# A seventh product in place of eight for SwiGLU's first pair, and a bank seeded by ScalarE

## The chip, the cores and the metric

The kernel runs on one core of one Trainium2 chip. The metric is the device time of one execution in microseconds (us), the median of several; one execution is profiled on its own. TensorE is called PE (PEld is its weight load), VectorE DVE, ScalarE ACT, GpSimd POOL, SyncE SP.

## What is computed

One layer of an encoder block on x of 512 tokens by 1024 features, all float32:

```python
h = rmsnorm(x, g_mix); proj = h @ w_in                       # 1024 -> 11264 columns
y_a = (gb * dwconv3(gc * xc)) @ w_a_out                      # gated short convolution
y_r = (groupnorm(retention(q, k, v)) * g_ret * silu(g_sw)) @ w_r_out
x = x + (sigmoid(gate_a) * y_a + sigmoid(gate_r) * y_r) @ w_o
h2 = rmsnorm(x, g_ffn)
x = x + (silu(h2 @ w_ff_gate) * (h2 @ w_ff_up)) @ w_ff_down  # 1024 -> 2816 -> 1024
return rmsnorm(x, g_final)
```

The stretch that matters here is the last matmul of the mixer (w_o) and the SwiGLU that follows it.

## The kernel before

Every float32 operand is held as two parts, hi and lo; a product of tiles is three matmuls (hi by hi, hi by lo, lo by hi). `split` makes the parts: ACT copies hi, then DVE subtracts it from the source to get lo (L171, L172).

Most matrix products go by a scheme of seven products in place of eight: a quad is a two by two arrangement of blocks of the weights (b11, b12, b21, b22) and of the activations. The seven weight units, in `FORMS`, are b11, t1, t2, b21, t3, t4, b22; t1 to t4 are sums of two blocks, and each of them costs one more DVE add (L244) ahead of its split. On the side of the activations four sums s1 to s4 are formed (`sums`, L602), four adds and four splits. `fm_quad` (the convolution's columns), `strassen` (the other projections and the down projection) and `pair` (SwiGLU's gate and up columns) each run the seven products into three banks of PSUM, called a, d and b: b11 into a, which ACT copies out as p1; t1 into d; t2 on top of a, copied out as u2; b21 into b, and DVE then adds p1 to it; t3 on top of a, copied out as u3; t4 on top of a; b22 on top of d. A product that adds to bank a can't start before the copy of a has read it.

SwiGLU has eleven such quads q = 0 to 10 of 256 gate and 256 up columns, and three parts of the down projection, after q = 2, 6 and 10 (`FF_PARTS`). One product of a SwiGLU quad is one call of `prod`: 24 matmuls of 128 x 256. The first quad is different: `first_pair` (L983) computes its eight products plainly from the four blocks, since the products for the first 256 tokens can start before the last quarter of the tokens has been turned (`tr_o`) and the sums s1 to s4 exist. For q = 1 `begin` and `second` (the products of b11 and b21) stand ahead of `pair`; for later quads `second(q)` stands between the products of t2 and t3, and `begin(q + 1)` between those of t3 and t4.

The weights come in the order of `PLAN`. `load_raws` issues the DMAs on SP's queue, `LEAD` = 4 units ahead, into ten raw buffers; `prefetch_form` makes the sum, if there is one, in place in its raw buffer, and splits it into one of five pairs of buffers (`wpool`); `take` hands the next unit out and keeps two more on the way (`AHEAD`).

The order in which each engine gets its instructions is not the text's: a planner sorts them ahead of time, by the order of the text, by what is ready by its own clock and by which buffers are free. So an add or a split for a later quad can stand ahead of work that the text puts first, and matmuls of one product between those of another.

Of the kernel before, what the change touches and what calls it, by code (L numbers as in the profile page):

```python
# [21 lines left out]
NB = S // P  # L22
# [33 lines left out]
def plan():  # L56
# [47 lines left out]

    f(0, "b11", "b21", "b12", "b22")
    f(1, "b11", "b21")
    for q0, n in FF_PARTS:
        for q in range(max(q0, 1), q0 + n):
            f(q, *(x for x in FORMS[1:5] if q > 1 or x != "b21"))
            if q + 1 < NQ:  # L110
                f(q + 1, "b11")
            f(q, "t4", "b22")
        units = [(name, u) for name in FORMS for u in range(0, n, 2)]
        if q0 + n == NQ:

            i = units.index(("b21", 2))
            units[i:i + 3] = units[i + 1:i + 3] + units[i:i + 1]
        for name, u in units:
            out.append(("q", ("d", q0), name, u, min(2, n - u)))
# [7 lines left out]
def loads():  # L127

    out = []
    for i, x in enumerate(PLAN):  # L130
        if x[0] == "q":
            _, quad, name, u, nk = x
            need = name if quad == ("f", 0) else NEEDS.get(name)
            if need:
                out.append((i, quad, need, u, nk * WIDTH[quad[0]]))
# [7 lines left out]
def block_kernel(ctx: ExitStack, tc: tile.TileContext, xT, xtok, wpack, wquad, cols, decs, rot, g_ffn, g_final, out):  # L143
# [173 lines left out]
    def prod(w, x, ps, start, stop=True):  # L317

        (wh, wl), (xh, xl) = w, x
        for s in range(2):  # L320
            o = ps[:, s * 256:(s + 1) * 256]
            for k in range(4):
                c = slice(k * 256 + s * P, k * 256 + (s + 1) * P)
                for i, (l, r) in enumerate(((wh, xh), (wh, xl), (wl, xh))):
                    nc.tensor.matmul(o, l[:, c], r[:, k], start=start and s == 0 and k == 0 and i == 0,  # L325
                                     stop=stop and k == 3 and i == 2, skip_group_check=True)

    def fm_quad(forms, ev11, ev21, ev22, ev12):

        def w():  # L330
            return take()[1][0]
        a, d, b = bank(), bank(), bank()
        prod(w(), forms["a11"], a, True)
        p1 = snap(a)
        prod(w(), forms["s1"], d, True)
        prod(w(), forms["s2"], a, False)
        u2 = snap(a)
        prod(w(), forms["a12"], b, True)
        nc.vector.tensor_tensor(out=p1, in0=b, in1=p1, op=ALU.add)
        ev11(p1)  # L340
        prod(w(), forms["s3"], a, False)
# [37 lines left out]
    def strassen(n, forms, ev11, ev21, ev22, ev12):  # L379


        a, d, b = ([bank(), bank()] for _ in range(3))
        prod_tm(n, forms["a11"], a, True)
        p1 = [snap(x) for x in a]
        prod_tm(n, forms["s1"], d, True)
        prod_tm(n, forms["s2"], a, False)
        u2 = [snap(x) for x in a]
        prod_tm(n, forms["a12"], b, True, True)
        for tt in range(2):
            nc.vector.tensor_tensor(out=p1[tt], in0=b[tt], in1=p1[tt], op=ALU.add)  # L390
            ev11(tt, p1[tt])
        prod_tm(n, forms["s3"], a, False)
# [58 lines left out]
    class SumSq:  # L451
# [18 lines left out]
        def rstd_tokens(self):  # L470
# [13 lines left out]
            for nb in range(NB):  # L484
                nc.vector.tensor_scalar_mul(diag[:, nb * P:(nb + 1) * P], ident, r[:, nb:nb + 1])
            self.diag = (t512(F32R), t512(F32R))
            split(diag, *self.diag)
            return r

        def rstd_row(self):  # L490

            ps = bank()
            nc.tensor.matmul(ps, ones_r, self.diag[0], start=True, stop=False)
# [131 lines left out]
    def do_quad(left, right, func, func_left=None):  # L625
# [6 lines left out]

        def ev21(tt, ps):
            t = t512()
            nc.scalar.activation(t, ps, func_left or AF.Copy)
            store(left[:, 2 + tt, :], t)
        strassen(4, xforms, ev_sum(left, 0, func_left), ev21, ev_sum(right, 2, func), ev_sum(right, 0, func))

# [289 lines left out]
    for nb in range(NB):  # L928
# [4 lines left out]
        if nb:  # L933
            tr_o(nb - 1, hs[nb - 1])
        hs[nb] = ev_o(nb, [po[half][nb] for half in range(2)])


# [44 lines left out]

    def first_pair():  # L983
        w = {}
        g0, u0, g1, u1 = bank(), bank(), bank(), bank()
        _, (w["b11"],) = take()
        prod(w["b11"], XF[0, 0], g0, True, False)
        _, (w["b21"],) = take()
        prod(w["b21"], XF[1, 0], g0, False)
        tr_o(NB - 1, hs[NB - 1])  # L990
        _, (w["b12"],) = take()
        prod(w["b12"], XF[0, 0], u0, True, False)
        _, (w["b22"],) = take()
        prod(w["b22"], XF[1, 0], u0, False)
        gated(0, 0, g0, u0)
        prod(w["b11"], XF[0, 1], g1, True, False)
        prod(w["b21"], XF[1, 1], g1, False)
        XF.update(sums(xf32[0, 0], xf32[1, 0], xf32[0, 1], xf32[1, 1]))
        prod(w["b12"], XF[0, 1], u1, True, False)
        prod(w["b22"], XF[1, 1], u1, False)  # L1000
        gated(0, 1, g1, u1)

    heads_of = {}

    def begin(q):
# [4 lines left out]
        prod(w, XF[0, 0], st["a"], True)  # L1010
        st["p1"] = snap(st["a"])

    def second(q):
        b = bank()
        _, (w,) = take()
        prod(w, XF[1, 0], b, True)
        g = heads_of[q]["p1"]
        nc.vector.tensor_tensor(out=g, in0=b, in1=g, op=ALU.add)

    def pair(q):  # L1020
# [12 lines left out]
        nc.vector.tensor_tensor(out=u3, in0=d, in1=u3, op=ALU.subtract)  # L1033
        if q + 1 < NQ:
            begin(q + 1)
# [16 lines left out]
    def down(n):  # L1052
        strassen(n, act_forms(), lambda tt, t: add_y(t, tt, 0), lambda tt, ps: add_y(snap(ps), 2 + tt, 0),
                 lambda tt, t: add_y(t, 2 + tt, 1), lambda tt, t: add_y(t, tt, 1))

    first_pair()
    begin(1)
    second(1)
    for q0, n in FF_PARTS:
        for q in range(max(q0, 1), q0 + n):  # L1060
            pair(q)
# [155 lines left out]
```

## Time and profile before

| | us |
|---|---|
| time, median of 3 runs | 1044.6 (1043.32 to 1044.88) |
| the profiled execution | 1043.97 |
| its span in the trace | 1042.2 |
| PE busy | 1028.3 (99%) |
| PEld busy | 897.0 (86%) |
| DVE busy | 875.5 (84%) |
| ACT busy | 523.4 (50%) |
| POOL busy | 107.7 (10%) |

The span is the trace's; the time of the execution has 1.8 us around it. The granted clock of PE is at its full share through the span but for the tail. SwiGLU's products begin at 702.06 us of the span; the eight of the first quad, with a turn of 1.00 us among them, end at about 726; the first part of the down projection begins at 769.53.

### The profile page before, as it was taken

The page shows a single profiled execution, that of the slowest core. Times are in us where ns is not written, and L with a number is a line of the kernel's source. Part 1 is how long each engine was busy: PE and PEld are TensorE (multiplying, and loading weights), DVE is VectorE, ACT ScalarE, POOL GpSimd, SP SyncE. Part 2 cuts the span into 40 slices and gives each one's busy share as a digit, 9 for nine tenths or more (in the row PEclk, how much of TensorE's full clock was granted, in tenths as well). Part 3 has the DMA queues.
Part 4 walks back from the last instruction along what each step waited for, and adds up shares of the span by engine and source line. Part 5 has one row for each costly group of instructions (what it writes and reads, how often), then busy time and mean ns, then how long its engine had stood idle before and what let it go on. Part 6 is the DMA issues. An engine that isn't in the chain of part 4 may idle for free.

```text
span 1042.2 us, 14832 instructions
## 1 busy us (share of the span) xinstructions
PE 1028.3 (99%) x5664; PEld 897.0 (86%) x5664; DVE 875.5 (84%) x1127; ACT 523.4 (50%) x698; POOL 107.7 (10%) x180
## 2 busy tenths in 40 slices
PE   8999999999999999999999999999999999999996
PEld 7788888888888998888888888889998999899985
DVE  6999786858787888697989998669998899889995
ACT  6546745452656545243443234355555565556553
POOL 0121111111111004202011000000002000110011
PEclk9999999999999999999999999999999999999999
DMA  9635638173645576919176535630319322663322
GB/s 325 223 117 201 236 123 281 71 254 119 199 141 182 169 284 233 341 42 358 42 283 247 205 111 173 236 113 28 92 45 275 117 85 78 193 152 102 122 35 87
DMA packets 49688, 175.07 MB, mean 168 GB/s; under 512 B 6480, under 2 KB 6480, under 8 KB 46288
## 3 DMA queue, kind: packets, MB, share of 16 engines
q1 hardware_dynamic: 36592, 131.12, 36.9%
q0 software_dynamic: 13024, 43.00, 12.9%
q8 instruction: 44, 0.72, 0.3%
q14 instruction: 28, 0.23, 0.1%
HBM read 135.56 MB, written 38.54 MB: 167 GB/s over the span
## 4 chain that ended last, share of the span: by engine, by line
PE 77%; issue 9%; DVE 7%; DMA 3%; POOL 2%; ACT 1%; SPq 0%; POOLq 0%; DVEq 0%; ACTq 0%
PE bank L369 29%; PE bank L325 27%; PE bank L285 7%; PE bank L284 7%; PE bank L286 7%; DVE wlo L172 1%; POOL z L566 1%; DVE big L185 1%; DMA big<-ql 1%; DMA big<-xT 1%; DMA z<-t 1%; DMA tab<-tab 0%; DVE big L172 0%; DVE t L464 0%; DVE big L175 0%
## 5 line engine op out<-in xcount | busy, mean ns | idle before, releaser
L171 ACT CAST whi<-raw 128x1024 fp32r<-128x1024 f32 (+1 forms) x281 | 288.6, 1032 | 302.7 <-PE bank L369 66.4
L172 DVE TENSOR_TENSOR wlo<-raw,whi 128x1024 fp32r<-128x1024 f32 (+1 forms) x281 | 335.8, 1202 | 108.8 <-ACT whi L171 107.8
L325 PE MATMUL bank<-xform,whi 128*128 128x256 f32 x1440 | 260.3, 283 | 0.0
L325 PEld LDWEIGHTS bank<-xform,whi 128*128 128x128 f32 x1440 | 224.8, 192 | 0.7 <-ACT t L376 0.6
L325 PE MATMUL bank<-xform,wlo 128*128 128x256 f32 x720 | 203.7, 283 | 0.0
L369 PE MATMUL bank<-whi,big 128*128 128x512 f32 x548 | 172.4, 390 | 0.0
L244 DVE TENSOR_TENSOR raw<-raw 128x1024 f32<-128x1024 f32 (+1 forms) x124 | 148.5, 1205 | 1.8 <-DMA raw<-wquad 0.4
L325 PEld LDWEIGHTS bank<-xform,wlo 128*128 128x128 f32 x720 | 138.2, 192 | 0.0
L369 PEld LDWEIGHTS bank<-whi,big 128*128 128x128 f32 x548 | 102.7, 188 | 22.4 <-DVE big L172 0.6
L369 PE MATMUL bank<-wlo,big 128*128 128x512 f32 x274 | 106.7, 389 | 0.0
L369 PE MATMUL bank<-whi,xform 128*128 128x512 f32 x320 | 101.2, 389 | 0.3 <-ACT t L376 0.3
L284 PE MATMUL bank<-whi,big 128*128 128x512 f32 x240 | 94.3, 395 | 1.8 <-ACT big L174 1.8
L285 PE MATMUL bank<-wlo,big 128*128 128x512 f32 x240 | 94.3, 393 | 0.0
L286 PE MATMUL bank<-whi,big 128*128 128x512 f32 x240 | 93.4, 392 | 0.0
L284 PE MATMUL bank<-big,whi 128*128 128x512 f32 x224 | 87.1, 389 | 0.0
L285 PE MATMUL bank<-big,whi 128*128 128x512 f32 x224 | 87.1, 389 | 0.0
L286 PE MATMUL bank<-big,wlo 128*128 128x512 f32 x224 | 87.1, 389 | 0.0
L376 ACT COPY t<-bank 128x512 f32<-128x512 f32 x96 | 55.5, 585 | 35.8 <-PE bank L369 17.2
L369 PEld LDWEIGHTS bank<-whi,xform 128*128 128x128 f32 x320 | 60.1, 188 | 13.1 <-ACT t L376 0.7
L369 PE MATMUL bank<-wlo,xform 128*128 128x512 f32 x160 | 62.2, 389 | 0.0
L369 PEld LDWEIGHTS bank<-wlo,big 128*128 128x128 f32 x274 | 51.4, 188 | 10.5
L284 PEld LDWEIGHTS bank<-whi,big 128*128 128x128 f32 x240 | 45.5, 190 | 12.5 <-ACT big L174 2.1
(173 smaller groups left out, 1398.6 us busy)
## 6 DMA issues: line engine op xcount, KB each, us to landing
raw<-wquad SPq DMA_DIRECT2D x124, 512.0 KB, 4.4
raw<-wpack SPq DMA_DIRECT2D x58, 512.0 KB, 4.9
z<-t POOLq DMA_DIRECT2D x24, 256.0 KB, 4.9
zform<-z POOLq DMA_DIRECT2D x6, 1024.0 KB, 6.2
v<-t POOLq DMA_DIRECT2D x16, 256.0 KB, 5.0
sg<-t POOLq DMA_DIRECT2D x16, 256.0 KB, 3.3
qh<-t POOLq DMA_DIRECT2D x16, 256.0 KB, 2.6
ql<-t POOLq DMA_DIRECT2D x16, 256.0 KB, 2.7
```

The costliest lines, as they stand in the source:

```text
L171: nc.scalar.copy(hi, src)
L172: nc.vector.tensor_tensor(out=lo, in0=src, in1=hi.bitcast(F32), op=ALU.subtract)
L185: nc.vector.transpose(o[:, :, :, b, :], i[:, :, :, q, :])
L244: nc.vector.tensor_tensor(out=t, in0=t, in1=raws[quad, more, u][:, 0:n], op=ALU.add)
L284: nc.tensor.matmul(ps, lh, rh, start=first, stop=False)
L285: nc.tensor.matmul(ps, lh, rl, start=False, stop=False)
L286: nc.tensor.matmul(ps, ll, rh, start=False, stop=last)
L325: nc.tensor.matmul(o, l[:, c], r[:, k], start=start and s == 0 and k == 0 and i == 0, stop=stop and k == 3 and i == 2, skip_group_check=True)
L369: nc.tensor.matmul(pss[tt], l, r[:, c], start=start and k == 0 and i == 0, stop=stop and k == n - 1 and i == 2, skip_group_check=True)
L376: nc.scalar.copy(t, ps)
L566: nc.gpsimd.dma_start(dst, t)
```

## The change

SwiGLU's quad 0 runs by seven products like the others. Ahead of it stand five products: b11 and b21 of quad 0, then (behind the last turn and the sums) b11 and b21 of quad 1, and b11 of quad 2; then `pair(0)` and `pair(1)`, each of five products with none of another quad in between in the text, then `pair(2)` with its seven as before. In every quad of the kernel (but the last part of the down projection, whose code stands apart) the product of b11 is now copied by ACT into the PSUM bank b (`seed`), and the product of b21 adds to that bank; DVE's add falls away, and what it fed reads the bank. For quads 0 to 2 of SwiGLU that bank is one that the w_o stage leaves. In the w_o stage two more units are fetched, after its second and its fourth block of tokens. The row of reciprocal norms at the start is made in the bank that its column was made in.

```diff
-    f(0, "b11", "b21", "b12", "b22")
+    f(0, "b11", "b21")
     f(1, "b11", "b21")
+    f(2, "b11")
     for q0, n in FF_PARTS:
-        for q in range(max(q0, 1), q0 + n):
+        for q in range(q0, q0 + n):
             f(q, *(x for x in FORMS[1:5] if q > 1 or x != "b21"))
-            if q + 1 < NQ:
+            if 1 < q < NQ - 1:
                 f(q + 1, "b11")
             f(q, "t4", "b22")
...
+    def seed(ps, t=None):
+        t = t or bank()
+        nc.scalar.copy(t, ps)
+        return t
...
-        a, d, b = bank(), bank(), bank()
+        a, d = bank(), bank()
         prod(w(), forms["a11"], a, True)
-        p1 = snap(a)
+        b = seed(a)
...
-        prod(w(), forms["a12"], b, True)
-        nc.vector.tensor_tensor(out=p1, in0=b, in1=p1, op=ALU.add)
-        ev11(p1)
+        prod(w(), forms["a12"], b, False)
+        ev11(b)
...
         def rstd_row(self):
-            ps = bank()
+            ps = self.ps
...
         hs[nb] = ev_o(nb, [po[half][nb] for half in range(2)])
+        if nb in (1, 3):
+            prefetch()
...
     def begin(q):
...
         prod(w, XF[0, 0], st["a"], True)
-        st["p1"] = snap(st["a"])
+        st["p1"] = seed(st["a"], (po[0][1], po[0][2], po[1][2])[q] if q < 3 else None)
     def second(q):
-        b = bank()
         _, (w,) = take()
-        prod(w, XF[1, 0], b, True)
-        g = heads_of[q]["p1"]
-        nc.vector.tensor_tensor(out=g, in0=b, in1=g, op=ALU.add)
+        prod(w, XF[1, 0], heads_of[q]["p1"], False)
     def pair(q):
...
-        if q + 1 < NQ:
+        if 1 < q < NQ - 1:
             begin(q + 1)
...
-    first_pair()
+    begin(0)
+    second(0)
+    tr_o(NB - 1, hs[NB - 1])
+    XF.update(sums(xf32[0, 0], xf32[1, 0], xf32[0, 1], xf32[1, 1]))
     begin(1)
     second(1)
+    begin(2)
     for q0, n in FF_PARTS:
-        for q in range(max(q0, 1), q0 + n):
+        for q in range(q0, q0 + n):
             pair(q)
```

`strassen` gets the same two edits as `fm_quad`, for both of its token tiles; `do_quad` and `down` evict the first result from PSUM by an ACT activation or copy, where they took it from SBUF.

## Rows read from the trace of the kernel before

**Rows 1.** The page's first part: engine, busy us, share, instructions.

```profile
PE 1028.3 (99%) x5664; PEld 897.0 (86%) x5664; DVE 875.5 (84%) x1127; ACT 523.4 (50%) x698; POOL 107.7 (10%) x180
```

**Rows 2.** Chain of waits in order of time, w_o's end to part one: start, us, what.

```profile
702.06 5.75 PE bank L325 x48
707.80 1.00 PE bank L910 x8
708.81 60.72 PE bank L325 x504
769.53 29.28 PE bank L369 x126
```

**Rows 3.** Busy time by stretch: length; busy (count) of PE, PEld, DVE, ACT, POOL; clock, DMA.

```profile
657.00:681.00 24.00, 24.00 (x115) 19.80 (x114) 11.14 (x13) 8.03 (x10) 0.00 (x0) 1.00 0.58 205
681.00:702.00 21.00, 21.00 (x107) 17.66 (x106) 13.61 (x26) 11.19 (x25) 1.64 (x3) 1.00 0.31 107
711.00:732.00 21.00, 21.00 (x177) 21.00 (x176) 19.80 (x24) 11.68 (x15) 0.00 (x0) 1.00 0.00 1
732.00:770.00 38.00, 38.00 (x314) 37.72 (x313) 36.07 (x44) 20.29 (x29) 0.00 (x0) 1.00 0.28 84
799.00:880.00 81.00, 81.00 (x675) 80.87 (x674) 76.01 (x92) 46.07 (x62) 1.75 (x2) 1.00 0.39 118
```

**Rows 4.** Groups by line and shape, whole span: busy us, mean ns, idle before, releasers.

```profile
L172 DVE TENSOR_TENSOR wlo<-raw,whi 128x1024 fp32r<-128x1024 f32 x270 | 328.4, 1223 | 101.9 <-ACT whi L171 101.0
L244 DVE TENSOR_TENSOR raw<-raw 128x1024 f32<-128x1024 f32 x120 | 145.8, 1223 | 1.8 <-DMA raw<-wquad 0.4
L376 ACT COPY t<-bank 128x512 f32<-128x512 f32 x96 | 55.5, 585 | 35.8 <-PE bank L369 17.2 <-PE bank L325 15.6 <-PE bank L286 2.5
L1018 DVE TENSOR_TENSOR t<-bank,t 128x512 f32<-128x512 f32 x10 | 6.9, 691 | 0.7 <-PE bank L325 0.7
L1033 DVE TENSOR_TENSOR t<-bank,t 128x512 f32<-128x512 f32 x10 | 6.9, 690 | 0.8 <-ACT t L376 0.8
L602 DVE TENSOR_TENSOR big<-big 128x1024 f32<-128x1024 f32 x8 | 9.8, 1220 | 0.0
```

**Rows 5.** DVE's instructions in order of time: start, us, what, count [idle before].

```profile
680.09 1.23 DVE L172 TENSOR_TENSOR wlo<-raw,whi 128x1024 fp32r<-128x1024 f32 x1 [4.21 <-ACT whi L171]
700.77 1.22 DVE L172 TENSOR_TENSOR wlo<-raw,whi 128x1024 fp32r<-128x1024 f32 x1
704.96 1.22 DVE L244 TENSOR_TENSOR raw<-raw 128x1024 f32<-128x1024 f32 x1
711.02 2.48 DVE L602 TENSOR_TENSOR big<-big 128x1024 f32<-128x1024 f32 x2
728.55 1.22 DVE L172 TENSOR_TENSOR wlo<-raw,whi 128x1024 fp32r<-128x1024 f32 x1
736.17 3.70 DVE L172 TENSOR_TENSOR wlo<-raw,whi 128x1024 fp32r<-128x1024 f32 x3
```

**Rows 6.** ACT's copies of bank a in quad 1, in order of time; same columns.

```profile
738.52 0.58 ACT L376 COPY t<-bank 128x512 f32<-128x512 f32 x1
742.33 0.59 ACT L376 COPY t<-bank 128x512 f32<-128x512 f32 x1 [3.23 <-PE bank L325]
```

**Rows 7.** PE's weight loads in order of time, behind the first of these copies.

```profile
739.15 0.30 PEld L325 LDWEIGHTS bank<-xform,whi 128*128 128x128 f32 x2 [0.20 <-ACT t L376]
```

**Rows 8.** Chain of waits in order of time, in the last quad.

```profile
989.63 1.61 PE bank L369 x7
991.24 5.95 PE bank L325 x48
```

**Rows 9.** Who waited for whom, PE's weight loads, whole span: total us, times, longest.

```profile
PEld bank L325 <- ACT t L376: 1.2, 5, 0.4
```

**Rows 10.** SP's DMA issues in order of time, the w_o stage.

```profile
658.96 22.72 SPq L232 DMA_DIRECT2D raw<-wquad  x7
682.00 19.20 SPq L884 DMA_DIRECT2D ydr<-big  x7
```

More of the change, by code (lines that the diff above doesn't have):

```diff
@@ L132, in loads @@
             _, quad, name, u, nk = x
-            need = name if quad == ("f", 0) else NEEDS.get(name)
+            need = NEEDS.get(name)
             if need:
@@ L379, in strassen @@
     def strassen(n, forms, ev11, ev21, ev22, ev12):
-        a, d, b = ([bank(), bank()] for _ in range(3))
+        a, d = ([bank(), bank()] for _ in range(2))
         prod_tm(n, forms["a11"], a, True)
-        p1 = [snap(x) for x in a]
+        b = [seed(x) for x in a]
         prod_tm(n, forms["s1"], d, True)
@@ L387, in strassen @@
         u2 = [snap(x) for x in a]
-        prod_tm(n, forms["a12"], b, True, True)
+        prod_tm(n, forms["a12"], b, False, True)
         for tt in range(2):
-            nc.vector.tensor_tensor(out=p1[tt], in0=b[tt], in1=p1[tt], op=ALU.add)
-            ev11(tt, p1[tt])
+            ev11(tt, b[tt])
         prod_tm(n, forms["s3"], a, False)
@@ L485, in rstd_tokens @@
                 nc.vector.tensor_scalar_mul(diag[:, nb * P:(nb + 1) * P], ident, r[:, nb:nb + 1])
+            self.ps = ps
             self.diag = (t512(F32R), t512(F32R))
@@ L631, in ev_sum, with ev_left, ev @@
             return ev
[L633 to L637, printed above, removed]
+        def ev_left(o):
+            def ev(tt, ps):
+                t = t512()
+                nc.scalar.activation(t, ps, func_left or AF.Copy)
+                store(left[:, o + tt, :], t)
+            return ev
+        strassen(4, xforms, ev_left(0), ev_left(2), ev_sum(right, 2, func), ev_sum(right, 0, func))
     for h in range(HEADS):
@@ L981, in gated @@
         both(2, w)
[L983 to L1001, printed above, removed]
     heads_of = {}
@@ L1052, in down @@
     def down(n):
-        strassen(n, act_forms(), lambda tt, t: add_y(t, tt, 0), lambda tt, ps: add_y(snap(ps), 2 + tt, 0),
+        strassen(n, act_forms(), lambda tt, ps: add_y(snap(ps), tt, 0), lambda tt, ps: add_y(snap(ps), 2 + tt, 0),
                  lambda tt, t: add_y(t, 2 + tt, 1), lambda tt, t: add_y(t, tt, 1))
-    first_pair()
+    begin(0)
+    second(0)
+    tr_o(NB - 1, hs[NB - 1])
+    XF.update(sums(xf32[0, 0], xf32[1, 0], xf32[0, 1], xf32[1, 1]))
     begin(1)
     second(1)
+    begin(2)
     for q0, n in FF_PARTS:
-        for q in range(max(q0, 1), q0 + n):
+        for q in range(q0, q0 + n):
             pair(q)
```

## The prediction, made before the change was run

> **What bounds the kernel now.** I read the page's busy times first: PE is busy for 1028.3 of 1042.2 us, with DVE next at 875.5 [rows 1]. A busy PE can hide waits, so I went on to the chain of waits around the change. There PE alone stands in it: two products from 702.06, a turn of 1.00 us, then 504 matmuls in 60.72 us without a break, then the down projection [rows 2]. 504 matmuls are 21 products of 24, so one product takes 2.88 to 2.89 us (48 in 5.75 us gives the same). PE is the bound of this stretch, it has no gaps to fill, and only fewer products or new gaps can change its end. The table of stretches shows who is next: DVE is busy 19.80 of 21 us (711 to 732) and 36.07 of 38 us (732 to 770), and 76.01 of 81 us in four later quads, so 19.0 us a quad against 7 x 2.88 = 20.2 us of PE [rows 3]. DVE has little room, and least of it where the change puts work.
>
> **The product that goes.** Quad 0 has seven products in place of eight: 24 matmuls, 2.88 us less of PE [rows 2], and all of it is on the path. That is 0.28% of the time, the most that this edit can give.
>
> **What DVE gets in exchange.** Quad 0 now needs seven units with four sums in place of four plain units: three more splits and four more adds. Each has a duration of 1.22 us [rows 4]; back to back three take 3.70 us and two of L602 take 2.48 [rows 5], so 1.24 us each, and seven make 8.7 us. The two subtractions of quad 0 that the seven products want add 2 x 0.69 (L1033) [rows 4]. The adds that fall away give back 0.69 each (L1018) [rows 4], two of them (quads 1 and 2) before 770. Sum: 8.7 + 1.4 - 1.4 = 8.7 us more DVE work, in a stretch that PE wants to leave 2.9 us sooner. DVE's room there is 1.2 + 1.9 = 3.1 us [rows 3]. It lacks 8.7 + 2.9 - 3.1 = 8.5 us. What covers it: in 657 to 702 DVE idles 12.9 + 7.4 us [rows 3], where adds can run in the raw buffers as soon as those have landed (in the kernel before one for a later quad ran at 704.96 [rows 5]); the raw loads are issued by 681 and SP's queue is then held by the ydr stores to 701 [rows 10], so what is loaded by then is all that can run early. Four adds, 4.9 us, fit. The rest, 3.6 us, comes from the lead that DVE had: counting units, its split at 728.55, done at 729.8, is t2 of quad 1, and by the count of products (six of quad 0, then b11, b21 and t1) that product starts at 708.81 + 9 x 2.88 = 734.7 [rows 2, 5], a lead of 5 us. So DVE keeps up, just; I take 0 for its lateness, and 0 to 2 us for the range.
>
> **The two units further ahead.** Splits need a pair of the five buffers. In the kernel before a split ran at 680.09 after DVE had idled, and the next one only at 700.77, when w_o's own units come free [rows 5], and one more behind it. Five units were thus ready for SwiGLU's start already, by the planner, which runs ahead of the text. The extra calls change which units these are and their rank, not their number: I cost them at nothing, between -1.2 us of DVE (one split earlier) and +1.2 us (one in the way of w_o's evictions). No SP wait is added; the DMAs of the two units stand ahead of the ydr stores as before.
>
> **The seed.** ACT copies a bank into a bank in place of a bank into SBUF; the trace shows no such write. The nearest row is 585 ns (L376) [rows 4]; as both ends I take half and twice that. b21's product now waits for that copy, where it waited for nothing. In quads from 2 on and in the other projections two products lie between, so the copy is covered more than five-fold. In quads 0 and 1 `second` follows `begin` at once: the wait is covered by products of the next `begin`, whose units are ready. Cost 0; without that cover 2 x 1.3 us. ACT's work grows by a copy for each of the few results that came from SBUF; it is busy for half of the span [rows 1]. DVE's 0.69 us a quad in later quads frees an engine that is not the bound: nothing.
>
> **The new waits.** `pair(0)` and `pair(1)` now run t1, t2, t3, t4, b22 with nothing of another quad between: t3 adds to bank a as soon as u2 is copied, and t4 as soon as u3 is. Before, only quad 1 had one such place (t2 to t3) and quad 10 another (t3 to t4), and the planner filled both: seven matmuls of the down projection, 1.61 us, stand in the last quad's [rows 8]; in quad 1, t2 ends by the count at 708.81 + 10 x 2.88 = 737.6, its copy starts at 738.52, and PE goes on with t3 at 739.15 [rows 2, 6, 7], so 1.5 us were filled from the product of b11 of quad 2, and 0.2 was lost. All such waits of the kernel together cost 1.2 us [rows 9], thanks to the fill. The price without fill: copy 0.59, 0.3 from the last matmul to the copy (742.0 to 742.33 [rows 6], by the same count), 0.1 to the weight load and 0.1 on to the matmul, so 1.1 us at least; with ACT in the middle of a split, up to 1.7, as in quad 1. I take 1.35. There are four places. The only fill is the next quad's t1 (b11 of quad 2 has been spent ahead). By DVE's order (from 711 on the eight sums and splits of s1 to s4, then t3's split, t4's add and split and b22's split, 12 x 1.24 = 14.9 us, then the split itself) quad 1's t1 is ready at about 727 to 728, too late for the places at 708.81 + 5 x 2.88 = 723.2 (b11 and b21 of quad 1, b11 of quad 2, t1, t2) and, one place and one product on, 727.4. Quad 2's t1 comes a quad of DVE's work later, 19.0 - 0.7 = 18.3 us less the 2.5 of two adds done early, about 743: too late for the first place of `pair(1)`, in time for the second. Three places open: 3 x 1.35 = 4.05 us.
> In this price the weight load counts for 0.1 us, since it waited for the copy too [rows 7]. The Trainium skill, "TensorE: Matmul & The Clock Gate", in "Architectural detail: the array is 16× 32×32, not 1× 128×128", says that PE's queue can pull a weight load ahead of matmuls in flight; by that the load would be done when the copy ends, a place would cost 1.25 and the sum would be +0.9 us. Rows 7 speak against it.
>
> **The sum.** -2.88 + 4.05 = +1.2 us. Made on the profiled execution, 1043.97 + 1.2 = 1045.2; that execution lies 0.6 below the median of the runs shown, and I forecast against the median: 1044.6 + 1.2 = 1045.8 us. The bank at the start (one less) is costed at nothing, -0.5 to +0.5: PE's waits there are for DVE's and ACT's work, which stays.
>
> **The rivals.**
> *All places are filled or covered* (1041.8 to 1042.5). If DVE runs the four adds early and quad 1's t1 is ready by 723, PE has matmuls at every place and loses 0.1 to 0.2 each, as in rows 7: -2.88 + 0.6 = -2.3, 1042.3. For it: DVE's 20 idle us before 702 [rows 3], and a planner that left 1.2 us of such waits in the whole kernel [rows 9]. Against: the five buffers. Chance 0.2.
> *Half filled* (1043.1 to 1044.6). One or two places open: -2.88 + 1.35 to 2.7. Chance 0.2.
> *DVE becomes the bound* (1047 to 1049.5, slower). t2's split needs a buffer that `second(0)` gives back at about 709, so it may fall behind the eight sums and splits of s1 to s4, 8 x 1.2 = 9.6 us from 711 [rows 4, 5]: ready at 722 where the product could start at 720.4. That costs 2 us, DVE is then late by as much at each later unit, no place is filled, and -2.88 + 2 + 4 x 1.35 = +4.5 gives 1049.1. It decides if the split isn't placed before 712. For it: the room that is missing. Against: a stalled PE gives DVE time. Chance 0.2.
> *The forecast*, three places and DVE in time, 1044.9 to 1046.8: chance 0.4.
> That the units further ahead don't come further ahead is a part of the forecast.
>
> **How the numbers follow.** About 0.2%, 2.1 us, is what a measurement here can tell from no change: faster is below 1042.5, slower above 1046.7. Faster: most of the first rival, 0.19. Slower: the third rival and a twentieth from the forecast's upper end, 0.25. Same: 0.56. The range reaches to the first rival's 1042.0 and the middle of the third's, 1048.4, and leaves out a tenth on each side.
>
> **What would show it.** Matmul count 5640. In the chain of waits, gaps of 1.1 to 1.7 us in front of L325 in 720 to 750, released by ACT's copies: three. A release by DVE's wlo there would be the third rival; matmuls of the next quad between t2 and t3 the first. DVE's L1018, L390 and L339 are gone. A change of over 1 us before 700, or after the first part of the down projection, would make the reasoning wrong: it would be the planner's.

## The result, and the profile after

| | before | after |
|---|---|---|
| median of 11 runs each, same chip (lowest to highest) | 1043.51 us (1042.38 to 1044.88) | 1046.55 us (1046.0 to 1047.25) |
| ratio, 95% interval | 1 | 1.0027 [1.0018, 1.0037] |
| profiled execution | 1043.97 us | 1046.29 us |

The changed kernel is slower by 3.0 us, 0.27%. The time lies in the range given; the likeliest of the three cases was "within 0.2%", and by the ratio what came is the slower one (chance 0.25). That 1046.55 also falls inside the forecast's own 1044.9 to 1046.8 is luck: those figures stand on a median of 1044.6, and on this chip the kernel before takes 1043.51, so that the forecast's +1.2 us would be 1044.7 here.

In the code after the change every line number of the part concerned is higher: L326 is the product that was L325, L333 the new seed, L376 the products of `strassen` (L369 before), L383 the copy to SBUF (L376 before), L172 and L173 the two halves of a split on ACT and DVE, L609 SwiGLU's sums.

The first part of the page (engine, busy us, share, instructions), to hold against [rows 1]:

```profile
PE 1027.3 (98%) x5640; PEld 894.4 (86%) x5640; DVE 868.7 (83%) x1107; ACT 534.5 (51%) x714; POOL 107.8 (10%) x180
```

24 matmuls are gone, as they should be, and PE's share has fallen by a point all the same: it waits more. The table of stretches says where (columns as in [rows 3]; the first two stretches are those of SwiGLU's first three quads, the third lies in later quads):

```profile
711.00:732.00 21.00, 19.06 (x149) 17.94 (x148) 20.02 (x20) 12.78 (x17) 0.00 (x0) 1.00 0.30 101
732.00:770.00 38.00, 37.56 (x311) 37.19 (x310) 36.35 (x49) 23.59 (x34) 0.00 (x0) 1.00 0.28 84
799.00:880.00 81.00, 81.00 (x670) 80.72 (x669) 74.25 (x86) 45.59 (x61) 2.02 (x3) 1.00 0.43 122
```

PE, which was busy for all of the 21 us from 711 [rows 3], now idles for 1.94 there and 0.44 in the next stretch; in later quads it is full. So I laid the two traces side by side by the starts of matmuls. From SwiGLU's first matmul to the first of the down projection it was 701.81 to 769.37 before, 67.56 us; it is 700.17 to 770.50 after, 70.34 us. The down projection's first part takes 30.09 us in place of 29.28. All that follows it takes the same to 0.1 us (234.77 after, 234.68 before). SwiGLU starts 1.65 us earlier in this profile. Sum: -1.65 + 2.78 + 0.81 + 0.09 = +2.03 at the last matmul, 1035.36 for 1033.33.

What happens in the first stretch is read from PE's weight loads. These are the ones that waited 0.16 us or more, in order of time (start, us, line and operation, and in brackets how long PE's loader had waited and for whom):

```profile
704.79 0.30 PEld L326 LDWEIGHTS bank<-xform,whi 128*128 128x128 f32 x2 [1.71 <-ACT bank L333]
713.33 0.30 PEld L326 LDWEIGHTS bank<-xform,whi 128*128 128x128 f32 x2 [0.31 <-ACT bank L333]
718.09 0.19 PEld L326 LDWEIGHTS bank<-xform,whi 128*128 128x128 f32 x1 [0.38 <-DVE xform L173]
722.19 0.62 PEld L326 LDWEIGHTS bank<-xform,whi 128*128 128x128 f32 x3 [1.18 <-ACT whi L172]
726.32 0.30 PEld L326 LDWEIGHTS bank<-xform,whi 128*128 128x128 f32 x2 [0.88 <-ACT t L383]
730.13 0.30 PEld L326 LDWEIGHTS bank<-xform,whi 128*128 128x128 f32 x2 [0.16 <-ACT t L383]
741.63 0.30 PEld L326 LDWEIGHTS bank<-xform,whi 128*128 128x128 f32 x2 [0.64 <-ACT t L383]
745.44 0.30 PEld L326 LDWEIGHTS bank<-xform,whi 128*128 128x128 f32 x2 [0.16 <-ACT t L383]
```

In order: `second(0)` waits for quad 0's seed, `second(1)` for quad 1's, quad 0's s1 product for the split of the sum, its t2, by the profile, for a cast of weights (what was late there was s2, as an experiment will show), then the four places behind a copy: t3 and t4 of quad 0, t3 and t4 of quad 1. Taken between starts of matmuls, with one 128x256 matmul (0.12) deducted, all such excess in the stretch was 0.64 us before and is 6.24 after: 5.6 more for a product of 2.88 less, which is the 2.8 us.

The chain of waits, one piece of PE in [rows 2], now runs over ACT and DVE (start, us, what):

```profile
712.81 0.68 DVE xform L924
713.49 1.13 DVE big L609
...
718.03 1.14 DVE big L609
...
719.20 1.05 ACT xform L172
720.25 1.90 ACT whi L172 x2
...
722.20 3.47 PE bank L326 x25
...
725.69 0.59 ACT t L383
...
726.32 14.65 PE bank L326 x118
```

From the last turn (L924) it goes through the sums, through ACT's cast of s2 and behind it two casts of weights, to t2's product; then over one copy.

And ACT in order of time, around the first seed, the first copy, and a seed in the down projection:

```profile
703.20 1.04 ACT L172 CAST whi<-raw 128x1024 fp32r<-128x1024 f32 x1 [0.53 <-PE bank L326]
704.15 0.58 ACT L333 COPY bank<-bank 128x512 f32<-128x512 f32 x1
...
725.69 0.58 ACT L383 COPY t<-bank 128x512 f32<-128x512 f32 x1 [2.59 <-PE bank L326]
...
775.08 0.57 ACT L333 COPY bank<-bank 128x512 f32<-128x512 f32 x1 [1.68 <-PE bank L376]
```

PE's last matmul ahead of the copy at 725.69 started at 725.37, so an idle ACT begins 0.32 us after that start, and PE lost 0.84 us. Ahead of the seed PE's last matmul started at 703.00; the copy could have begun at 703.32, but a cast of weights had begun at 703.20, and the copy ran at 704.15. The wait is 1.66: the same 0.83, and as much for the cast ahead of it in ACT's queue. That a queue of ACT is served strictly in order is what the Trainium skill says ("TensorE: Matmul & The Clock Gate", "Architectural detail: the array is 16× 32×32, not 1× 128×128"); these rows agree.

### The profile page after: what moved, and what is told of

Its sections match the earlier page's. It is cut to its first block, busy times and chain, and to the rows that moved or that the text cites. A ratio compares the mean times of both kernels' runs of the same rounds, so it can differ in the third digit from the quotient of the medians.

```text
span 1044.5 us, 14760 instructions
## 1 busy us (share of the span) xinstructions
PE 1027.3 (98%) x5640; PEld 894.4 (86%) x5640; DVE 868.7 (83%) x1107; ACT 534.5 (51%) x714; POOL 107.8 (10%) x180
## 4 chain that ended last, share of the span: by engine, by line
PE 78%; issue 9%; DVE 7%; DMA 3%; ACT 2%; POOL 1%; SPq 0%; POOLq 0%; DVEq 0%; ACTq 0%
PE bank L376 31%; PE bank L326 25%; PE bank L287 7%; PE bank L286 7%; PE bank L285 7%; DMA z<-t 1%; DVE big L186 1%; DVE wlo L173 1%; DMA big<-ql 1%; POOL z L573 1%; DMA big<-xT 1%; ACT whi L172 0%; DVE big L173 0%; DVE big L781 0%; DVE big L176 0%
## 5 line engine op out<-in xcount | busy, mean ns | idle before, releaser
L172 ACT CAST whi<-raw 128x1024 fp32r<-128x1024 f32 (+1 forms) x284 | 291.8, 1032 | 301.1 <-PE bank L376 59.7
L173 DVE TENSOR_TENSOR wlo<-raw,whi 128x1024 fp32r<-128x1024 f32 (+1 forms) x284 | 338.9, 1199 | 125.8 <-ACT whi L172 124.4
L326 PE MATMUL bank<-xform,whi 128*128 128x256 f32 x1424 | 258.8, 284 | 3.9 <-ACT bank L333 1.5
L326 PEld LDWEIGHTS bank<-xform,whi 128*128 128x128 f32 x1424 | 222.2, 192 | 6.1 <-ACT t L383 2.2
L326 PE MATMUL bank<-xform,wlo 128*128 128x256 f32 x712 | 200.8, 283 | 0.0
L376 PE MATMUL bank<-whi,big 128*128 128x512 f32 x548 | 172.8, 390 | 0.5 <-ACT bank L333 0.4
L245 DVE TENSOR_TENSOR raw<-raw 128x1024 f32<-128x1024 f32 (+1 forms) x128 | 153.1, 1202 | 1.6
L326 PEld LDWEIGHTS bank<-xform,wlo 128*128 128x128 f32 x712 | 136.3, 192 | 0.0
L376 PEld LDWEIGHTS bank<-whi,big 128*128 128x128 f32 x548 | 102.7, 188 | 23.5 <-ACT bank L333 0.9
L376 PE MATMUL bank<-wlo,big 128*128 128x512 f32 x274 | 106.7, 389 | 0.0
L376 PE MATMUL bank<-whi,xform 128*128 128x512 f32 x320 | 100.9, 389 | 0.0
L376 PEld LDWEIGHTS bank<-whi,xform 128*128 128x128 f32 x320 | 60.1, 188 | 12.4
L383 ACT COPY t<-bank 128x512 f32<-128x512 f32 x73 | 42.7, 586 | 42.2 <-PE bank L326 22.1
L376 PE MATMUL bank<-wlo,xform 128*128 128x512 f32 x160 | 62.2, 389 | 0.0
L376 PEld LDWEIGHTS bank<-wlo,big 128*128 128x128 f32 x274 | 51.5, 188 | 10.5
```

The costliest lines, as they stand in the source:

```text
L172: nc.scalar.copy(hi, src)
L173: nc.vector.tensor_tensor(out=lo, in0=src, in1=hi.bitcast(F32), op=ALU.subtract)
L245: nc.vector.tensor_tensor(out=t, in0=t, in1=raws[quad, more, u][:, 0:n], op=ALU.add)
L376: nc.tensor.matmul(pss[tt], l, r[:, c], start=start and k == 0 and i == 0, stop=stop and k == n - 1 and i == 2, skip_group_check=True)
L383: nc.scalar.copy(t, ps)
```

## The experiments

All were timed in turns with the kernel before on the same chip; chips differ by up to a microsecond, so ratios are compared, not medians. "Stretch" is the time from SwiGLU's first matmul to the down projection's first, "excess" the sum of PE's waits in it, "part one" the length of the down projection's first part, all by the starts of matmuls in the traces.

| kernel | ratio to before, 95% | stretch | excess | part one |
|---|---|---|---|---|
| before | 1 | 67.56 | 0.64 | 29.28 |
| the change | 1.0027 [1.0018, 1.0037] | 70.34 | 6.24 | 30.09 |
| no units further ahead | 1.0040 [1.0025, 1.0055] | 70.35 | 6.22 | 30.10 |
| seeds in SwiGLU alone | 1.0015 [1.0005, 1.0025] | 70.34 | 6.22 | 29.01 |
| seeds everywhere but in SwiGLU | 1.0021 [1.0012, 1.0031] | 68.77 | 4.73 | 31.17 |
| seeds alone, quad 0 by eight | 1.0000 [0.9991, 1.0008] | 67.75 | 0.91 | 30.05 |
| starting bank alone | 0.9986 [0.9976, 0.9995] | 67.53 | 0.62 | 29.14 |
| seven products, no seeds | 1.0012 [1.0003, 1.0020] | 68.76 | 4.73 | 29.13 |
| seeds in any bank | 1.0042 [1.0029, 1.0055] | 71.21 | 7.1 | 30.07 |
| four adds less on DVE | 1.0032 [1.0019, 1.0044] | 69.56 | 5.49 | 30.07 |
| places filled by the text | 1.0057 [1.0043, 1.0072] | 72.04, two products more | 2.09 | 28.92 |
| first products and turn first | 1.0027 [1.0016, 1.0037] | 69.32 | 5.30 | 30.22 |
| s2 ahead of s3 | 1.0021 [1.0013, 1.0030] | 69.48 | 5.38 | 29.92 |
| three of these together | 1.0007 [0.9998, 1.0015] | 68.73 | 4.70 | 29.11 |

### The parts, one at a time

**Seeds in SwiGLU alone.** `fm_quad`, `strassen`, `do_quad` and `down` as before the change:

```diff
-        b = [seed(x) for x in a]
+        p1 = [snap(x) for x in a]
...
-        prod_tm(n, forms["a12"], b, False, True)
+        prod_tm(n, forms["a12"], b, True, True)
...
+            nc.vector.tensor_tensor(out=p1[tt], in0=b[tt], in1=p1[tt], op=ALU.add)
```

> The change, but with the seed taken out of fm_quad and strassen (p1 copied to SBUF and added by DVE, as before); SwiGLU as changed. Theory 1 (the seed holds a second bank for a quad that waits, so the down projection's products find none free and wait for the copy): the 0.8 us lost in the first part of the down projection comes back, about 1045.7 us. Theory 2 (those 0.8 us are the planner's order, not the banks): no change from the changed kernel, 1046.5 us, and the first part stays at 30.1 us against 29.3 before.

Part one is back at 29.01 us, 1.08 less than with seeds, and nothing in the first stretch moved. The loss of part one is the seeds'. In the trace of the change its place is this weight load:

```profile
775.70 0.19 PEld L376 LDWEIGHTS bank<-whi,big 128*128 128x128 f32 x1 [0.86 <-ACT bank L333]
```

The seed's copy ran at 775.08 (above) right behind the first product, and the product that adds to it stood next in the planner's order.

**Seeds everywhere but in SwiGLU.** The counterpart: `second` into a bank of its own, and DVE's add back.

```diff
-        st["p1"] = seed(st["a"], (po[0][1], po[0][2], po[1][2])[q] if q < 3 else None)
+        st["p1"] = snap(st["a"])
...
+        b = bank()
...
-        prod(w, XF[1, 0], heads_of[q]["p1"], False)
+        prod(w, XF[1, 0], b, True)
...
+        nc.vector.tensor_tensor(out=g, in0=b, in1=g, op=ALU.add)
```

> The change, but SwiGLU's p1 goes to SBUF and DVE adds it, as before; quad 0 still by seven products. Theory 1 (second waits for the seed, and no bank is free for another product to fill that wait): the 1.7 us wait ahead of b21 of quad 0 goes, and the three kept banks are free; the waits for the copies of bank a stay: about 1044.8 us. Theory 2 (DVE is the bound in this stretch): DVE has 0.7 us more in each quad, so nothing is gained, 1046.5 to 1048 us.

The seed waits are gone and the stretch is 1.57 us shorter, but 4.73 us of waits stay in it, and 1.08 of the gain is given back in part one: there PE waits 1.69 us for ACT's cast of an activation, where the change waited 0.46, and then 0.86 for the seed as before.

```profile
773.26 0.19 PEld L376 LDWEIGHTS bank<-whi,big 128*128 128x128 f32 x1 [1.69 <-ACT big L172]
```

An early arrival alone doesn't cost this. In "seven products, no seeds", below, PE reaches part one as soon (769.18 us for 769.08) and ACT casts that activation at the same time (772.70 for 772.59), but PE has 18 matmuls of part one to run ahead of the wait, where here it has 12, and waits 0.34:

```profile
773.37 0.19 PEld L377 LDWEIGHTS bank<-whi,big 128*128 128x128 f32 x1 [0.34 <-ACT big L172]
```

So this loss in part one, too, comes with the seeds outside SwiGLU, which leave PE fewer products to go on with. Whether the banks that they hold or the planner's order is the reason isn't shown.

**Seeds alone, quad 0 by eight products.** The kernel before with every seed and the starting bank, but `first_pair` kept; of the edit, here against the kernel before, lines of `second`:

```diff
-        prod(w, XF[1, 0], b, True)
-        nc.vector.tensor_tensor(out=g, in0=b, in1=g, op=ALU.add)
+        prod(w, XF[1, 0], heads_of[q]["p1"], False)
```

> The kernel before with the seed everywhere and the one bank at the start, but quad 0 by eight products and no further units ahead. Theory 1 (quad 0's seven products are what costs): 0.8 us for the down projection's first part and up to 1.3 us at second(1), less what the start gives: 1043.5 to 1045 us, and the stretch of SwiGLU's first three quads at 67.6 to 69 us. Theory 2 (the seeds cost it all): 1046 us or more.

The stretch is 67.75 (before: 67.56) and part one 30.05. With eight products in quad 0 the seeds find their cover in SwiGLU, and cost 0.8 us in part one alone. (The ratio, 1.0000, has the starting bank in it.)

**The starting bank alone.**

```diff
+            self.ps = ps
...
-            ps = bank()
+            ps = self.ps
```

> The kernel before with one edit: the row of reciprocal norms is made in the bank of its column. Theory 1 (the bank lets products go ahead of the row, so PE's wait of 2.1 us there shrinks): 1042.1 us. Theory 2 (that wait differs from run to run, with the first loads): 1043.5 us, no change.

1042.77 us for 1043.97, 0.14% faster [0.05, 0.24]; it is the one part of the change that pays, and this kernel the only one here that is faster than the kernel before. It was timed alone on one chip, and its interval only just leaves out no change. The weight load of the second matmul at that place (L494 before, L495 here) starts at 34.23 us of the span where it started at 35.04:

```profile
32.52 0.19 PEld L494 LDWEIGHTS bank<-t,ones_r 128*128 128x128 f32 x1 [0.64 <-ACT t L171]
34.23 0.19 PEld L495 LDWEIGHTS bank<-t,ones_r 128*128 128x128 f32 x1 [0.49 <-DVE t L172]
```

In the profile of before the first of these waited 2.14 us. In the profiles of the other twelve kernels that keep the bank (the change among them) that wait lies between 0.57 and 1.96, and the second load starts between 33.74 and 35.09. So one execution differs from another there by as much as the edit can be worth, and where the gain lies isn't shown by the profiles; that there is one rests on the timed runs. SwiGLU starts at 699.70 to 701.40 us in the thirteen profiles with the bank, and at 701.81 in the one without; that fits a gain, but one profile without the bank can't prove it.

**Seven products, no seeds.** The change without any seed; units ahead and starting bank kept.

> The change without any seed: p1 goes to SBUF and DVE adds it in every quad, as before; quad 0 by seven products, five products ahead, the further units and the one bank at the start stay. Theory 1 (seeds cost by waits and held banks, seven products by waits for the copies of bank a): the wait ahead of b21 of quad 0 and the loss in the down projection's first part are both gone, the four places between t2, t3 and t4 stay at 3 to 4 us, against 2.9 us less of products: 1044 to 1045.3 us. Theory 2 (the seeds are not the matter, DVE is): as with the seed out of SwiGLU alone, 1046.4 us or more.

Slower than before by 1.2 us, with 4.73 us of waits in the stretch, among them:

```profile
719.83 0.19 PEld L326 LDWEIGHTS bank<-xform,whi 128*128 128x128 f32 x1 [1.00 <-DVE xform L173]
723.51 0.30 PEld L326 LDWEIGHTS bank<-xform,whi 128*128 128x128 f32 x2 [0.88 <-ACT t L384]
...
727.32 0.30 PEld L326 LDWEIGHTS bank<-xform,whi 128*128 128x128 f32 x2 [0.22 <-ACT t L384]
...
739.59 0.30 PEld L326 LDWEIGHTS bank<-xform,whi 128*128 128x128 f32 x2 [0.70 <-ACT t L384]
...
743.40 0.30 PEld L326 LDWEIGHTS bank<-xform,whi 128*128 128x128 f32 x2 [0.88 <-ACT t L384]
```

One wait for the sums, and all four places behind a copy: 0.88, 0.22, 0.70 and 0.88. (One more, 0.36 for a cast of weights, stood between the first two of these.) So even without a seed the product that was saved isn't gained. From the stretch alone (+1.2 us against before) and from the medians against the starting bank alone (1.0012 over 0.9986, +2.7 us, each known to about 1 us) the seven products by themselves cost between 1 and 3 us.

**No units further ahead.**

```diff
-        if nb in (1, 3):
-            prefetch()
```

> The changed kernel without the two calls that ask for one unit of weights further ahead each. Theory 1 (a unit further ahead does nothing, because the buffers of the splits are already full at that place): the time of the changed kernel within 0.5 us (1046.0 to 1047.0), the waits of the first SwiGLU stretch the same within 0.3 us each. Rival (the earlier loads fill SwiGLU's start): the first product of SwiGLU or the second waits 1 to 3 us longer, 1047.5 to 1049.5.

Every wait of the stretch is the same to 0.01 us (1.66, 0.27, 0.34, 1.13, 0.83, 0.60 at the six that exceed 0.25), the stretch 70.35. The ratio, 1.0040, is above that of the change, but the intervals overlap, and this profile's lag against the change (0.93 us at SwiGLU's start) is there, but for 0.14, at 77 us already (77.42 for 76.63), long ahead of the edit. In the trace the calls do nothing.

### What fills or closes the places

**Seeds in any bank.** The theory was that the three kept banks tie the planner's hands. Quads 0 to 2 seed any free bank; part of their result can then come without the first product.

```diff
-        st["p1"] = seed(st["a"], (po[0][1], po[0][2], po[1][2])[q] if q < 3 else None)
+        st["p1"] = seed(st["a"])
```

> The change, but the seeds of SwiGLU's quads 0 to 2 take any bank that is free in place of banks kept from the w_o stage. What an earlier use left in such a bank may decide whether the product adds to the seed, so a part of quads 0 to 2 can come out without their first product. Theory 1 (the kept banks leave no bank for b11 of quad 1, which could fill the wait for the seed): the 1.7 us ahead of b21 of quad 0 shrinks below 0.5, about 1045.2 us. Theory 2 (the planner's rank keeps b11 of quad 1 behind the turn, whatever the banks): 1046.5 us.

The wait for the first seed is the same 1.71, the second is 1.27 in place of 0.31, and the stretch is 0.87 longer. The theory falls.

```profile
712.86 0.30 PEld L326 LDWEIGHTS bank<-xform,whi 128*128 128x128 f32 x2 [1.27 <-ACT bank L333]
```

**Four adds less on DVE.** Quad 0's products t1 to t4 take plain blocks, so that DVE has 4.9 us less to do.

```diff
-        if more:
+        if more and quad != ("f", 0):
```

> The change, but the four adds that make quad 0's units t1 to t4 are left out (quad 0 is computed from the plain blocks there), so DVE has 4.9 us less in the stretch. Theory 1 (waits for ACT's copies and seeds): the waits ahead of b21 of quad 0 (1.7) and of t3 (0.8 and 0.6) stay, those for the splits (1.2 and 0.4) shrink: 1045 to 1046 us. Theory 2 (DVE is the bound): most of the 5.7 us of waits goes, 1043 us or less.

DVE's total is not what is late: 4.9 us less of it shorten the stretch by 0.78 and leave the time where it was (1.0032 for 1.0027). The seed's wait (1.71) and t2's (1.10 for 1.18) are almost unchanged, and a new one, for the weights of a product behind t2, appears; the planner has ordered DVE's splits of weights anew:

```profile
722.10 0.63 PEld L326 LDWEIGHTS bank<-xform,whi 128*128 128x128 f32 x3 [1.10 <-ACT whi L172]
725.94 0.19 PEld L326 LDWEIGHTS bank<-xform,wlo 128*128 128x128 f32 x1 [0.59 <-DVE wlo L173]
```

**Places filled by the text.** Seven products without seeds, and a product of a later quad written between t2 and t3 and between t3 and t4, through quad 8 (the list of units and `pair` share this table):

```diff
+BETWEEN = {0: (("b21", 2), ("b11", 3)), 1: (("b21", 3), None), 2: (None, ("b11", 4)),
+           9: (("b21", 10), None), 10: (None, None)}
+BETWEEN.update({q: (("b21", q + 1), ("b11", q + 2)) for q in range(3, 9)})
```

> As the change without any seed, but with products of later quads between t2 and t3 and between t3 and t4 from quad 0 on: b21 of quad 2 and b11 of quad 3 in quad 0, b21 of quad 3 in quad 1, b11 of quad 4 in quad 2, then b21 of q + 1 and b11 of q + 2, up to quad 8; quad 9 has one and quad 10 none. Theory 1 (the waits are those for the copies of bank a, and plain units are what DVE can make in time): the waits in the first three quads fall from 3 to 4 us to under 1.5, so 1041.5 to 1043 us, below the kernel before. Theory 2 (DVE is the bound of the stretch, whatever the order): no better than without this order, 1044 to 1046 us.

The stretch holds two products more (5.76 us); without them it is 72.04 - 5.76 = 66.28, 2.5 us under the same kernel unfilled. Excess is 2.09 for 4.73. At the three copy places of quads 0 and 1 that have a product between no wait is left; the two that the table leaves empty, t3 to t4 of quad 1 and t2 to t3 of quad 2, still wait:

```profile
749.09 0.30 PEld L335 LDWEIGHTS bank<-xform,whi 128*128 128x128 f32 x2 [0.57 <-ACT t L393]
761.53 0.30 PEld L335 LDWEIGHTS bank<-xform,whi 128*128 128x128 f32 x2 [0.87 <-ACT t L393]
```

So the places are open where no product of another quad stands between. But running a quad further ahead costs more later: from part one's end to the second down projection it takes 5.0 us longer than before, and what follows 1.9 us less with two products (5.76 us) less to do, so that 3.9 us were lost there as well. The first of these waits and DVE's row beside it:

```profile
804.78 0.29 PEld L335 LDWEIGHTS bank<-xform,wlo 128*128 128x128 f32 x1 [2.76 <-DVE wlo L182]
```

```profile
795.55 2.48 DVE L254 TENSOR_TENSOR raw<-raw 128x1024 f32<-128x1024 f32 x2
802.36 1.23 DVE L254 TENSOR_TENSOR raw<-raw 128x1024 f32<-128x1024 f32 x1 [4.34 <-DMA raw<-wquad]
```

DVE itself waited 4.34 us for a load. Why the load came late, a raw buffer still held or its place in the queue, wasn't settled.

### Repairing the start

**First products and turn first.** The order `begin(0)`, `begin(1)`, the last turn and the sums, `second(0)`, `second(1)` (`PLAN` has its units in the same order):

```diff
     begin(0)
-    second(0)
+    begin(1)
     tr_o(NB - 1, hs[NB - 1])
     XF.update(sums(xf32[0, 0], xf32[1, 0], xf32[0, 1], xf32[1, 1]))
-    begin(1)
+    second(0)
     second(1)
```

> The changed kernel with another order of SwiGLU's start: the first products of pairs 0 and 1, then the last turn and the eight sums, then the second products of pairs 0 and 1. Theory 1 (the seed waits of 1.66 and 0.27 us are missing cover, and the sums are late because the last turn stands behind a product that waits for a seed): both seed waits under 0.3 us, the waits for the sums (0.34 and 1.14) under 0.5 together, first SwiGLU stretch 70.3 -> 67.0 to 68.3 us, median 1043.3 to 1045. Rival (the start is bound by VectorE's and ScalarE's work between the turn and t2 whatever TensorE's order): the seed waits go, but the waits before t1 and t2 grow by as much, the stretch stays 69.8 to 70.6 and the time 1046 to 1047.

Both seed waits are gone, t2's is gone, s1's is 0.53, as theory 1 has it; but the time is not better, because the copy places now stand open:

```profile
719.58 0.19 PEld L328 LDWEIGHTS bank<-xform,whi 128*128 128x128 f32 x1 [0.53 <-DVE xform L175]
723.26 0.30 PEld L328 LDWEIGHTS bank<-xform,whi 128*128 128x128 f32 x2 [0.88 <-ACT t L385]
727.08 0.30 PEld L328 LDWEIGHTS bank<-xform,whi 128*128 128x128 f32 x2 [0.64 <-ACT t L385]
739.29 0.30 PEld L328 LDWEIGHTS bank<-xform,whi 128*128 128x128 f32 x2 [0.88 <-ACT t L385]
...
743.93 0.30 PEld L328 LDWEIGHTS bank<-xform,whi 128*128 128x128 f32 x2 [1.60 <-ACT t L385]
```

Together 4.00 us, where the same four cost 1.84 in the change. Neither theory as written: the waits moved, not to the sums as the rival had it, but to the copies.

**s2 ahead of s3.** In SwiGLU's call of `sums` alone; `new` is a buffer that it gets for this:

```diff
-                ("s1", a22, a21, a22, ALU.subtract), ("s3", a21, a11, a21, ALU.subtract),
-                ("s2", a11, a22, a11, ALU.subtract), ("s4", a12, a12, a11, ALU.add)):
+                ("s1", a22, a21, a22, ALU.subtract), ("s2", new, a22, a11, ALU.subtract),
+                ("s3", a21, a11, a21, ALU.subtract), ("s4", a12, a12, new, ALU.add)):
```

> The changed kernel with SwiGLU's sums in the order s1, s2, s3, s4 (s2 into a buffer of its own, so that it needn't follow s3): s2's halves are ready one sum and one split (2.3 us on VectorE) earlier, with the same work on every engine. Theory 1 (t2's wait of 1.14 us is the place of s2 in the serial chain of sums and splits): that wait under 0.2 us, s3's product not late, for its place follows 4 us behind: first stretch 70.3 -> 69.0 to 69.4, median 1045.2 to 1045.6. Rival (t2 waits for its weights' split on ScalarE and VectorE, not for s2): the wait stays 0.9 to 1.3 and the time 1046.2 to 1046.9.

t2's wait of 1.18 is gone, with the same work on every engine: what was late there was s2's place in the chain of sums, though the profile names the cast of weights (L172), which stood behind s2's cast in ACT's queue. DVE's times agree: in the change its subtraction for s2 began at 721.36 and took 1.22 us, to 722.58, and the third matmul of that place started at 722.63. The stretch is 0.86 shorter, and the copies take back 0.6:

```profile
725.63 0.30 PEld L326 LDWEIGHTS bank<-xform,whi 128*128 128x128 f32 x2 [0.64 <-ACT t L383]
729.45 0.30 PEld L326 LDWEIGHTS bank<-xform,whi 128*128 128x128 f32 x2 [0.16 <-ACT t L383]
741.02 0.30 PEld L326 LDWEIGHTS bank<-xform,whi 128*128 128x128 f32 x2 [0.72 <-ACT t L383]
...
744.83 0.30 PEld L326 LDWEIGHTS bank<-xform,whi 128*128 128x128 f32 x2 [0.88 <-ACT t L383]
```

**Three together.** This order of sums, the first products and the turn first, and seeds in SwiGLU alone.

> The changed kernel with three edits together: the seeds taken out of the other quads and the down parts (as in the run of that name), the first products of pairs 0 and 1 and the last turn ahead of the second products, and s2 ahead of s3. If the losses found add up: 1046.55 - 0.8 (seeds) - 1.9 (seed waits) - 1.0 to 1.5 (sums) = 1042.3 to 1042.9, first stretch 66.8 to 67.6, which is at or under the kernel before (1043.5) and about the kernel before with the starting bank kept (1042.8). If something else is late in their place (the copies between u2 and t3, weights): 1043.5 to 1045, and the wait that takes their place is seen in the first stretch.

1.0007 [0.9998, 1.0015]: most of the loss is repaired, but a gain on the kernel before isn't shown. No seed and no sum is waited for (one cast of weights is, 0.34 us). The stretch is 68.73, not 66.8 to 67.6, and of its 4.70 us the four copy places make 3.8 with the 0.10 behind each. The loader's waits at them are 3.6 together:

```profile
722.28 0.30 PEld L328 LDWEIGHTS bank<-xform,whi 128*128 128x128 f32 x2 [0.88 <-ACT t L386]
...
726.10 0.30 PEld L328 LDWEIGHTS bank<-xform,whi 128*128 128x128 f32 x2 [0.24 <-ACT t L386]
738.30 0.30 PEld L328 LDWEIGHTS bank<-xform,whi 128*128 128x128 f32 x2 [0.88 <-ACT t L386]
...
742.95 0.30 PEld L328 LDWEIGHTS bank<-xform,whi 128*128 128x128 f32 x2 [1.60 <-ACT t L386]
```

The last of them is a copy behind casts once more: PE's last matmul started at 741.27, so that the copy could have begun at 741.59; ACT ran two casts from 740.42, and the copy began at 742.32.

```profile
740.42 1.99 ACT L174 CAST whi<-raw 128x1024 fp32r<-128x1024 f32 x2 [2.17 <-DVE raw L247]
742.32 0.58 ACT L386 COPY t<-bank 128x512 f32<-128x512 f32 x1
```

## Why the prediction was right and wrong, step by step

- **The product that goes, -2.88.** Right: 24 matmuls fewer, 0.12 us each. All of it was on the path, and all of it was lost again.
- **The new waits, +4.05.** The mechanism is right, the price and the number are off, both to the high side. An open place costs 0.83 and another 0.10 behind the next matmul, 0.93 us, not 1.35, with ACT free; with a cast ahead in ACT's queue 1.66. Of the four places one was fully open in the change, one in part, two were filled to 0.2: 0.94 + 0.70 + 0.22 + 0.22 = 2.1 us. Why fewer: the seeds and the sums had held PE up ahead of them, and in that time, as I read it, the units that fill them became ready; what the runs show is the exchange. Where these holds were taken away (first products and turn first), the four cost 4.2 us with the 0.10 each: about the term of the sum, by another price and another count. Filling the places by the text took 2.5 us off the stretch and left waits for copies at the empty ones alone, which shows that missing products are the cause.
- **The seed, 0.** This step failed. The prediction said that "the wait is covered by products of the next `begin`, whose units are ready"; the planner kept `second(0)` right behind `begin(0)`, and the bound for missing cover, 2 x 1.3 us, was nearer: 1.66 + 0.27, and 0.1 behind each, 2.1 us. That "two products lie between" elsewhere failed at one place: the first part of the down projection pays 0.8 to 1.1 us, where the planner had put the adding product next, and 2.0 with seeds there and none in SwiGLU (31.17 for 29.13). The copy of a bank into a bank had been given half to twice 585 ns; it is as long as the nearest row.
- **DVE's lateness, 0 (0 to 2).** Wrong within its bounds: s1's wait is 0.34 and t2's 1.14, with the small gaps behind them 1.8 us. Not DVE's load, which I had added up unit by unit (4.9 us less of it took 0.78 off the stretch and nothing off the time), but the order of a serial chain: turn, four sums, their casts on ACT, and weights' casts behind them. In the third rival I had t2 held up for 2 us, to 722, by the split of its weights behind the sums. t2 was late, and to 722.2, but not for that reason: one move in the order of the sums took the wait away. That DVE is then late at each later unit didn't come either.
- **Units further ahead, 0.** Right: without the calls the same waits to 0.01 us.
- **The bank at the start, -0.5 to +0.5.** Outside its bounds, to the good side: -1.2 us by itself, though the interval, -2.5 to -0.5, touches them.
- **The sum.** Written anew by the trace of the change, from SwiGLU's start on: -2.88 for the product, +2.1 copies, +2.1 seeds, +1.8 sums, less the 0.6 of waits that were there before and with 0.3 in small gaps, +2.8 in the stretch; +0.8 in part one. With -1.65 at the start that is +2.0 in the profiles and +3.0 in the medians; the remaining microsecond is within what two single executions differ by, and I assign it to nothing. That the prediction's +1.2 came within 2 us of this was luck in part: its copies were 2.0 too dear, which stood in for half of the 3.9 that seeds and sums cost, and the seeds' 0.8 in part one ran against the earlier start.
- **What would have shown it.** I asked for three gaps of 1.1 to 1.7 us behind ACT's copies in 720 to 750; there were two, 0.96 and 0.72 between starts, and the largest gap stood at 703, ahead of the window. "A change of over 1 us before 700" came too: SwiGLU starts 1.65 us earlier. The starting bank is one cause that was found, but one profile against one can't tell it from what differs between executions.

What stays open: why the planner leaves `second(0)` behind its seed while, by the count of splits, the first product of another quad is ready to run (the kept banks aren't it), and why running a quad further ahead delays later loads.

## What to carry to other kernels

Fewer products for the engine that bounds the kernel are worth nothing where the products that go were the ones that covered the others' waits: count, for the shorter schedule, what stands between each bank's last product, its copy and the next product that adds to it. Waits in one queue that hide behind each other don't add up: here 4.7 to 6.2 us stayed in the stretch whichever of seeds, sums or DVE work was taken out, and only products put between removed them. When an edit bundles several parts, time each alone: the one that paid here was two lines about a bank at the start.

## What the runs showed of the hardware

ACT's copy from bank to bank takes as long as one from bank to SBUF. The two lines over the whole span (count, then min, median and max in ns):

```profile
L333 ACT COPY bank<-bank x30: 550/577/613, 81.7 to 975.2; 128x512 f32<-128x512 f32 x30
```

```profile
L383 ACT COPY t<-bank x73: 571/587/596, 35.5 to 992.5; 128x512 f32<-128x512 f32 x73
```

577 and 587 ns. The Trainium skill ("ScalarE: Activation LUTs", "Step-by-step: what each stage is for") has PSUM as the faster target of the two; by these rows it is faster by 2%, and nothing in the time hangs on it. And the weight load waits with its matmul: in each row of PE's weight loads above, the first load behind a copy starts when the copy has ended (the one of 725.69, 0.58 long, and the load at 726.32), so that the 1.25 us that the pull-ahead would have made of a place isn't what these rows show; the place is cheaper than I had it for other reasons. The copy began 0.32 us after the last matmul's start, which is 0.2 behind its slot of 0.12 where I had 0.3; and the load and its matmul started together (both at 726.32), 0.05 behind the copy's end (726.27), where I had put 0.1 for the one and 0.1 more for the other.
